# Splitting attention queries and keys where they are projected instead of where they are used

## The chip, the cores and the metric

The kernel runs on one core of a Trainium2 chip. The metric is the device time of one execution in microseconds (us). Before the change three executions took 3174.82, 3191.3 and 3205.16 us; the median is 3191.3.

## The reference, cut to what matters

One inference step of a one-layer trunk: a joint input projection, forgetting attention (8 heads of 64) and an mLSTM (4 heads of 128) side by side, an output projection, layer norm and a squared-ReLU MLP. It is done for a prompt of 2048 tokens and for 8 sequences of 8 sampled tokens whose keys and values lie in a paged cache of 8192 tokens each. All is float32. The part around the change is the prompt's attention:

```python
z = jnp.einsum('bsd,dc->bsc', x, w_in)
fq = z[..., OFF_FOX_Q:OFF_FOX_K].reshape(B, S, FOX_HEADS, FOX_HEAD_DIM)
fk = z[..., OFF_FOX_K:OFF_FOX_V].reshape(B, S, FOX_HEADS, FOX_HEAD_DIM)
...
L = jnp.cumsum(logf, axis=1).transpose(0, 2, 1)
...
s = jnp.einsum('bqhd,bkhd->bhqk', q_i, k).astype(jnp.float32) * scale
s = s + L_i[..., :, None] - L[:, :, None, :]
s = jnp.where(k_pos[None, :] <= q_pos[:, None], s, -jnp.inf)
p = jax.nn.softmax(s, axis=-1)
return jnp.einsum('bhqk,bkhd->bqhd', p.astype(v.dtype), v)
```

The keys `fk` are an output of their own too (`k_prompt`).

## The kernel before

**Three terms for one product.** Where float32 accuracy is wanted, an operand `x` is split into `hi` (rounded to the format fp32r) and `lo = x - hi`. `split_hi` (L154) is a copy on ScalarE, `split_lo` (L157) a subtraction on VectorE. `mm3` (L163 to L165) multiplies hi by hi, hi by lo and lo by hi.

**Phases.** Phase A (`block_a`) projects the tokens in four blocks of 512 (the first block with the 64 sampled tokens as well), in passes over columns of `w_in`: values and gates of the mLSTM, its queries and keys with a short convolution, output gates, then the attention's queries and keys (loop from L610, `j` 0 to 3 queries, 4 to 7 keys), then its values. For queries and keys a tile of PSUM has 128 columns by up to 512 tokens. In L632 to L635 ScalarE copies it in pieces of 256 tokens to `st` (queries scaled by 1/8) and SP's queue stores each piece: queries to the scratch tensor `dq` in DRAM, keys to the output `k_prompt`. PSUM tiles of this pool rotate over four banks.

Beside phase A run, woven in by `tick`, the mLSTM (`m_block`) and the attention over the cache (`sample_attention`), whose gathers are DMAs of the POOL queue: keys `kT` (L2109), values `vt`, `vx` or `y` (L2221); TensorE uses them in L2132 and L2245. `m_block` loads the end-of-chunk decays `gsb` (L738) and takes their exponential on ScalarE right away (L741), ahead of the loop over chunks; `gsb` is used in L793, at the end of a chunk. The gates `gm` are copied in L463; `m_load` (L714) waits for them with its load of `Wq`.

**Phase B** (`phase_b`, from L976) is the prompt's attention, in 64 units: 8 heads `h` by 8 groups `g` of 256 queries. The main loop does `scores` of unit n and then `values` of unit n - 1 (`LA = 1`).

- Keys: `keys_load` fetches 64 rows by 512 tokens twice, into both halves of the 128 partitions of `kn`; `keys` makes `ks` of it, hi on partitions 0 to 63 and lo on 64 to 127 (one `split_hi`, one `split_lo` on half the partitions). One matmul with `qh` on both halves then gives `qh*(hi + lo)`. Two tensors `ks0`, `ks1` of 2048 tokens alternate between heads.
- Queries: `queries_load` fetches 64 rows by 256 tokens twice into `qn`, two units ahead; `queries` makes `qh` and `ql`, one unit ahead.
- Scores: two matmuls (L1042, L1043) per query tile and 512 keys into a bank `pS` (three in turn); VectorE adds the negative cumulated forget gate `nl` while it copies the scores to `S` and takes the row maximum (L1050, L1054). For the tile on the diagonal the addend is `nd = nl + mask`, made on POOL (L1035) just before it is used, three buffers.
- Values: ScalarE takes the exponential (L1071), TensorE transposes (L1087), ScalarE or VectorE copies to `PT` (L1090, L1092), TensorE multiplies by the values `vn` (L1097) into `po`, which goes to `ot` (L1105, L1107). `nl` (1 MB, broadcast over partitions) and `vn` (512 KB, in rows of 256 bytes) of a head are loaded whole (`forget_values`, L984, L985) at g = 3 of the head before; head 0's come in quarters.
- `ot` holds 64 rows by 1024 queries, two buffers. When a half of a head is through, `finish` puts three steps into the list `ends`, of which the main loop does one per unit: `stores` of the inverse sums to DRAM (L1122), `sums`, which loads them broadcast (`rl`, L1128), and `scale`, two multiplications `ot*rl` and their stores to `dmix` (L1133, L1134). They run on POOL and SP's queue; at the very end (`end`) the first of the two runs on VectorE and the stores are POOL's, and the list is emptied in one go.

**Order.** The program is written in the order above, but each engine's order is made by a scheduler that simulates a timeline (`schedule_with_timeline_sim=True`): an instruction whose operands and buffer are there may go ahead of earlier ones. Each engine and queue then takes its instructions in the order so made, so an issue on SP's queue that waits has the later loads and stores behind it. POOL issues the cache gathers and, in phase B, the sums of weights of the MLP (`w2_sum`, L1242).

**Behind phase B** the output projection `phase_o` loads operands from `dmix` (`mix`, `xr`, L1318), splits them (`mh`, `ml`), loads residual rows `y` (L1345) and weights `w_o` in pieces (`half_wo`, L1247: five buffers `wr`, split into `wh`, `wl` for the first half of the columns and `woh`, `wol` for the second), and multiplies in L1359. Its tiles lie in memory that phase B used.

```python
ends.extend([stores, sums, scale])
while end and ends:
    ends.pop(0)()
```

## Time and profile before

| what | us |
|---|---|
| median of three executions | 3191.3 |
| the profiled execution | 3166.91 |
| its span, first to last instruction | 3165.1 |
| TensorE busy in the span | 3076.4 |
| phase A, to the first scores | 864.9 |
| phase B, first scores to last values | 440 |
| the rest: output projection, MLP | 1860 |

PE is TensorE's matmul, PEld its loading of the stationary operand, DVE is VectorE, ACT is ScalarE, POOL is GpSimd, and SP is the engine that issues most DMAs; a `q` behind an engine's name stands for its sequencer, which waits and issues. A group row reads: line, engine, operation, `out<-in` by the program's names, shape, count, then busy us and mean ns of one, then the idle us of the engine just before them and what ended it. A row of a window gives the stretch, its length, each engine's busy us (and instructions), the granted share of TensorE's clock, the mean busy share of the 16 DMA engines and GB/s. A row of waits reads: who waited, for whom, us in total, times, the longest. A row of a timeline gives start, duration, engine, line, operation and, in brackets, the idle time before it and what ended it; neighbours of one kind are merged (`x4`).

### The profile page before, as it was taken

The page shows a single profiled execution, that of the slowest core. Times are in us where ns is not written, and L with a number is a line of the kernel's source. Part 1 is how long each engine was busy: PE and PEld are TensorE (multiplying, and loading weights), DVE is VectorE, ACT ScalarE, POOL GpSimd, SP SyncE. Part 2 cuts the span into 40 slices and gives each one's busy share as a digit, 9 for nine tenths or more (in the row PEclk, how much of TensorE's full clock was granted, in tenths as well). Part 3 has the DMA queues.
Part 4 walks back from the last instruction along what each step waited for, and adds up shares of the span by engine and source line. Part 5 has one row for each costly group of instructions (what it writes and reads, how often), then busy time and mean ns, then how long its engine had stood idle before and what let it go on. Part 6 is the DMA issues. An engine that isn't in the chain of part 4 may idle for free.

```text
span 3165.1 us, 53757 instructions
## 1 busy us (share of the span) xinstructions
PE 3076.4 (97%) x19713; PEld 2425.7 (77%) x19713; DVE 2125.0 (67%) x5095; ACT 1457.3 (46%) x2648; POOL 961.5 (30%) x1046
## 2 busy tenths in 40 slices
PE   8999999999999999899999999999999999999998
PEld 8997787787766676677777777776777776798886
DVE  6857557466487888544566668665676656787888
ACT  4343244334377777422334354443454444455552
POOL 0121232333333334376423334324333222111110
PEclk9999999999999999999999999999999999999999
DMA  5565775777787787487977778978778866587772
GB/s 193 152 212 179 238 234 188 277 267 250 238 269 196 210 211 172 159 303 261 359 277 271 279 274 302 344 263 315 282 280 325 317 226 238 156 266 200 210 203 77
DMA packets 332512, 765.36 MB, mean 242 GB/s; under 512 B 64057, under 2 KB 154681, under 8 KB 331353
## 3 DMA queue, kind: packets, MB, share of 16 engines
q1 hardware_dynamic: 236120, 414.41, 39.9%
q0 software_dynamic: 90864, 330.61, 31.4%
q10 hardware_dynamic: 5264, 16.91, 1.4%
q8 instruction: 156, 2.56, 0.3%
q14 instruction: 108, 0.88, 0.1%
HBM read 709.23 MB, written 93.98 MB: 254 GB/s over the span
## 4 chain that ended last, share of the span: by engine, by line
PE 76%; DMA 11%; issue 5%; DVE 5%; POOL 2%; ACT 1%; SPq 0%; DVEq 0%; POOLq 0%; ACTq 0%
PE py L163 6%; PE py L165 6%; PE ph L163 6%; PE ph L165 6%; PE py L164 6%; PE ph L164 6%; PE pw L1359 5%; PE pm L163 5%; PE pm L165 5%; PE pm L164 5%; DMA y<-cache_v,idxV 3%; PE sO L2245 3%; PE po L1097 3%; DMA vt<-cache_v,idxV 3%; PE sQ L2132 3%
## 5 line engine op out<-in xcount | busy, mean ns | idle before, releaser
L157 DVE TENSOR_TENSOR wl<-wr,wh 128x1024 fp32r<-128x1024 f32 x321 | 393.5, 1230 | 237.3 <-ACT wh L154 235.7
L154 ACT ACTIVATE wh<-wr 128x1024 fp32r<-128x1024 f32 x321 | 337.6, 1055 | 326.0 <-PE ph L164 168.9
L2109 POOL DMA_INDIRECT kT<-cache_k,idxK x256 | 276.5, 1080 | 642.7 <-PE sQ L2132 576.4
L163 PE MATMUL py<-wh,hh 128*128 128x512 f32 x904 | 357.6, 400 | 0.1
L164 PE MATMUL py<-wl,hh 128*128 128x512 f32 x904 | 353.7, 393 | 0.0
L165 PE MATMUL py<-wh,hl 128*128 128x512 f32 x904 | 352.6, 394 | 0.8 <-DVE hl L157 0.8
L1668 DVE TENSOR_TENSOR y<-y,py 128x512 f32<-128x512 f32 x404 | 272.4, 681 | 84.5 <-PE py L165 81.4
L163 PE MATMUL ph<-x1h,wh 128*128 128x512 f32 x768 | 303.8, 396 | 0.0
L2221 POOL DMA_INDIRECT vt<-cache_v,idxV x197 | 203.2, 1032 | 329.8 <-PE sO L2245 257.4
L164 PE MATMUL ph<-x1l,wh 128*128 128x512 f32 x768 | 301.5, 393 | 0.0
L165 PE MATMUL ph<-x1h,wl 128*128 128x512 f32 x768 | 299.9, 393 | 0.0
L163 PE MATMUL pm<-xh,whi 128*128 128x512 f32 (+2 forms) x640 | 231.0, 361 | 0.0
L165 PE MATMUL pm<-xh,wlo 128*128 128x512 f32 (+2 forms) x640 | 228.8, 357 | 0.0
L164 PE MATMUL pm<-xl,whi 128*128 128x512 f32 (+2 forms) x640 | 227.9, 356 | 0.0
L163 PE MATMUL pm<-whi,xh 128*128 128x256 f32 (+4 forms) x624 | 202.1, 325 | 8.0 <-ACT whi L154 8.0
L157 DVE TENSOR_TENSOR wlo<-wra,whi 128x1024 fp32r<-128x1024 f32 (+1 forms) x112 | 141.0, 1261 | 101.1 <-ACT whi L154 100.8
L163 PEld LDWEIGHTS py<-wh,hh 128*128 128x128 f32 x904 | 169.4, 188 | 50.0 <-issue 5.9
L165 PEld LDWEIGHTS py<-wh,hl 128*128 128x128 f32 x904 | 170.1, 188 | 41.5 <-issue 4.9
L164 PE MATMUL pm<-wlo,xh 128*128 128x256 f32 (+4 forms) x624 | 199.5, 320 | 0.6 <-DVE wlo L157 0.6
L165 PE MATMUL pm<-whi,xl 128*128 128x256 f32 (+4 forms) x624 | 199.9, 320 | 0.0
L164 PEld LDWEIGHTS py<-wl,hh 128*128 128x128 f32 x904 | 170.5, 189 | 35.2 <-issue 2.5
L154 ACT ACTIVATE hh<-hq 128x512 fp32r<-128x512 f32 x150 | 94.1, 631 | 215.4 <-PE py L164 150.6
(442 smaller groups left out, 7210.5 us busy)
## 6 DMA issues: line engine op xcount, KB each, us to landing
wr<-w SPq DMA_DIRECT2D x214, 512.0 KB
wra<-w_in SPq DMA_DIRECT2D x104, 512.0 KB
wr<-dw SPq DMA_DIRECT2D x97, 512.0 KB
dw<-w POOLq DMA_DIRECT2D x63, 512.0 KB, 8.6
wr<-w POOLq DMA_DIRECT2D x34, 512.0 KB, 8.4
Rb<-dR SPq DMA_DIRECT2D x128, 128.0 KB
wx<-dw SPq DMA_DIRECT2D x17, 512.0 KB
xn<-xp_t SPq DMA_DIRECT2D x16, 512.0 KB
```

Of the source, the lines that this page charges most:

```text
L154: last["ACT"] = A.activation(dst, src, AF.Copy, scale=scale)
L157: r = (eng or V).tensor_tensor(dst, src, hi.bitcast(F32), op=OP.subtract)
L163: T.matmul(ps, wh, xh, start=first, stop=False, skip_group_check=shared)
L164: T.matmul(ps, wh, xl, start=False, stop=False, skip_group_check=shared)
L165: last["PE"] = T.matmul(ps, wl, xh, start=False, stop=stop, skip_group_check=shared)
L1097: last["PE"] = T.matmul(po[c:c + 64, q0:], z["vn"][:, k], PTs[k // 4][:, k % 4, q0:], start=(k < 2), stop=(k >= nk - 2), skip_group_check= ...
L1359: last["PE"] = T.matmul(ps, m[t][x][:, k], (wh, wl)[w][hf][k], start=i == 0, stop=i == 23)
L1668: V.tensor_tensor(y, y, ps, op=op)
L2109: G.indirect_dma_start(out=piece(n), out_offset=None, in_=ck, in_offset=IO(ap=idxK[:, b, j // 2, j % 2:j % 2 + 1], axis=0))
L2132: r = T.matmul(pq[h4 * 32:h4 * 32 + 32, hg].rearrange("p (k c) -> p k c", k=2), z["qb"][:, hd], kv, start=(db == 0), stop=(db == 1), skip_ ...
L2221: vx["last"] = G.indirect_dma_start(out=vt.rearrange("p f c -> p (f c)"), out_offset=None, in_=cv, in_offset=IO(ap=idxV[:, b, (kt % 4) * 4 ...
L2245: after_ = T.matmul(po[r:r + 32], z["PT"][:, hg, 2 * f + g, pg].rearrange("p h q -> p (h q)"), vts[f][:, g, hg * 256:(hg + 1) * 256], star ...
```

## The change

1. The projection stores queries and keys already split. ScalarE makes `hi` from PSUM (512 tokens at once where the tile has them), VectorE `lo` in one operation out of PSUM (`ps*scale - hi`), and SP stores both: queries to `dq[2, 512, S]`, keys to a new scratch tensor `dk[2, 512, S]`. The output `k_prompt` is still written as before, by its own two copies. The staging tiles are those that the convolution and the wide passes use (`ac`, `qi`).
2. Phase B loads the split form: `keys_load` brings hi and lo straight into `ks`, `queries_load` brings hi and lo of 256 queries into both halves of the partitions. `keys`, `queries` and their splits are gone. Five buffers `q` take the place of `qn`, `qh`, `ql`; loads run up to four units ahead.
3. `diagonals` makes a unit's two `nd` one unit ahead, with six buffers; for the first two units on VectorE.
4. `forget_values` of the next head comes in four pieces, at g = 4 to 7.
5. `ot` has three buffers, `ends` has an empty step between `sums` and `scale`, and at the very end both multiplications run on VectorE.
6. `gsb`'s exponential is taken in the first chunk of a block, after its outputs, instead of ahead of the loop.

```diff
-    dq = drm.tile([4, 128, S], F32, name="dq")
+    dq = drm.tile([2, 512, S], F32, name="dq")
+    dk = drm.tile([2, 512, S], F32, name="dk")
...
-                for o in range(w % 256, w, 256):
-                    st = pa.tile([128, 256], F32, name="st", bufs=4)
-                    A.activation(st, ps[:, o:o + 256], AF.Copy, scale=scale)
-                    SY.dma_start(O["k_prompt"][jj * 128:(jj + 1) * 128, a:a + 256] if c else dq[jj, :, a:a + 256], st)
+                n = w // 256 * 256
+                two = [lambda: pa.tile([128, 512], F32, name="sa", tag="ac", bufs=2),
+                       lambda: pa.tile([128, 512], F32, name="sq", tag="qi", bufs=2)]
+                if w == 512:
+                    hi, lo = (x().bitcast(F32R) for x in two)
+                else:
+                    x = two[w == 256]().bitcast(F32R)
+                    hi, lo = x[:, :256], x[:, 256:]
+                A.activation(hi, ps[:, w - n:], AF.Copy, scale=scale)
+                V.scalar_tensor_tensor(lo, ps[:, w - n:], scale, hi.bitcast(F32), op0=OP.mult, op1=OP.subtract)
+                for d, x in enumerate((hi, lo)):
+                    SY.dma_start((dk if c else dq)[d, jj * 128:(jj + 1) * 128, a:a + n], x.bitcast(F32))
+                for o in range(w - n, w, 256):
+                    if c:
+                        st = pa.tile([128, 256], F32, name="st", bufs=4)
+                        A.copy(st, ps[:, o:o + 256])
+                        SY.dma_start(O["k_prompt"][jj * 128:(jj + 1) * 128, a:a + 256], st)
                     a += 256
...
-        A.activation(gsb, gsb, AF.Exp)
         for c in range(bi * 4, bi * 4 + 4):
...
+            if c % 4 == 0:
+                A.activation(gsb, gsb, AF.Exp)
             Cn = pm.tile([128, 4, 129], F32, name="Cs", bufs=2)
...
+        def keys_load(z, g):
+            h = z["h"]
             for d in range(2):
-                SY.dma_start(kn[d * 64:d * 64 + 64], kp[h * 64:h * 64 + 64, g * 512:(g + 1) * 512])
-            return kn
+                SY.dma_start(z["ks"][g][d * 64:d * 64 + 64].bitcast(F32), dk[d, h * 64:h * 64 + 64, g * 512:(g + 1) * 512])
...
+            q = qs.pop() if qs else pb.tile([128, 2, 256], F32R, name="q", bufs=5)
+            for d in range(2):
+                SY.dma_start(q[d * 64:d * 64 + 64].bitcast(F32), q_of(*units[n]))
+            return q
...
+        def diagonals(n):
             h, g = units[n]
+            for qt in (2 * g, 2 * g + 1):
+                nd = nds[h, qt] = pb.tile([128, 128], F32, name="nd", bufs=6)
+                x = Z[h]["nl"][:, qt * 128:qt * 128 + 128]
+                if n < 2:
+                    V.tensor_tensor(nd, x, dmask, op=OP.add)
+                else:
+                    last["POOL"] = G.tensor_tensor(nd, x, dmask, op=OP.add)
...
-                z["ot"] = pb.tile([64, 1024], F32, name="ot", bufs=2)
+                z["ot"] = pb.tile([64, 1024], F32, name="ot", bufs=3)
...
-                    (V if end and q == 0 else G).tensor_tensor(ot[:, s], ot[:, s], rls[q], op=OP.mult)
+                    (V if end else G).tensor_tensor(ot[:, s], ot[:, s], rls[q], op=OP.mult)
...
-            ends.extend([stores, sums, scale])
+            ends.extend([stores, sums, lambda: None, scale])
...
+                if n + 1 < len(units):
+                    diagonals(n + 1)
                 if ends:
                     ends.pop(0)()
-                if n + 2 < len(units):
-                    qnext[n + 2] = queries_load(n + 2)
...
+                while max(qnext) < min(n + 4, 2 * n + 3, len(units) - 1):
+                    m = max(qnext) + 1
+                    qnext[m] = queries_load(m)
...
+                if h < 7 and g >= 4:
+                    forget_values(Z[h + 1], g * 512 - 2048, 512)
```

More of the change, by code (lines that the diff above doesn't have):

```diff
@@ L1030, in scores @@
                 mx = pb.tile([128, 8], F32, name="mx", bufs=6)
-                nd = pb.tile([128, 128], F32, name="nd", bufs=3)
-                if z["h"] == 0 and g < 2:
-                    V.tensor_tensor(nd, nl[:, qt * 128:n], dmask, op=OP.add)
-                else:
-                    last["POOL"] = G.tensor_tensor(nd, nl[:, qt * 128:n], dmask, op=OP.add)
+                nd = nds.pop((z["h"], qt))
                 st = []
@@ L1153, in phase_b @@
         dmask = bf["mask"]
-        keys(Z[0], 0, bf["kn"])
+        forget_values(Z[0], 0, 512)
+        nds = {}
+        diagonals(0)
         sc = {}
-        qnext = {1: queries_load(1)}
-        knext = {}
+        qnext = {0: bf["q"], 1: queries_load(1), 2: queries_load(2)}
         w2_due = [0.0]
```

95 lines of the change are left out of this document (34 added, 61 removed).

## The prediction

> **What bounds the kernel now.** I read the page first, then stretches of the span, then the waits of TensorE, then the places where these lie.
>
> ```profile
> span 3165.1 us, 53757 instructions
> PE 3076.4 (97%) x19713; PEld 2425.7 (77%) x19713; DVE 2125.0 (67%) x5095; ACT 1457.3 (46%) x2648; POOL 961.5 (30%) x1046
> q1 hardware_dynamic: 236120, 414.41, 39.9%
> ```
>
> TensorE is busy for 97%, and the change removes no matmul. It can win only what TensorE idles, or runs at a lower granted clock, near the code that it touches. The attention over the prompt (phase B) lies from 864.9 to 1304.9 us:
>
> ```profile
> core 0: us, PE busy (x) PEld busy (x) DVE busy (x) ACT busy (x) POOL busy (x), PEclk, DMA share, GB/s
> 864.90:904.90 40.00, 34.43 (x195) 22.73 (x196) 33.88 (x138) 29.26 (x71) 11.79 (x18) 0.91 0.74 207
> 1004.90:1024.90 20.00, 17.26 (x113) 12.34 (x113) 11.04 (x40) 11.12 (x25) 4.94 (x7) 0.91 0.69 152
> 1044.90:1064.90 20.00, 17.22 (x103) 11.60 (x103) 15.90 (x55) 12.25 (x29) 9.01 (x14) 0.91 0.75 205
> 1144.90:1184.90 40.00, 40.00 (x283) 28.82 (x282) 32.93 (x132) 29.01 (x68) 16.95 (x25) 1.00 0.90 222
> 864.90:1304.90 440.00, 422.22 (x2882) 296.64 (x2883) 352.14 (x1379) 331.42 (x769) 163.31 (x251) 0.98 0.75 199
> 1317.60:1337.60 20.00, 11.07 (x52) 7.79 (x52) 4.27 (x4) 3.17 (x3) 2.42 (x3) 0.83 1.03 402
> ```
>
> The fourth row shows the stage without trouble: all busy, full clock. Three stretches lose: idle 5.57, 2.74 and 2.78 us, and 0.09 of the clock, which is 3.6, 1.8 and 1.8 us. Over phase B that is 17.8 us of idle and 7.2 us of clock: **25 us is the most that B can give back.** The last row lies behind B, where the output projection starts: 8.9 us idle and 0.17 x 20 = 3.4 us of clock.
>
> **Phase B, part by part.** What TensorE waits for there:
>
> ```profile
> PE pt L1087 <- DVE PT L1092: 3.2, 4, 2.4
> PE pS L1042 <- DVE mx L1050: 2.8, 2, 1.4
> PE po L1097 <- DVE ot L1107: 2.7, 1, 2.7
> ```
>
> *Splits.* The splitting of queries and keys leaves B:
>
> ```profile
> L157 DVE TENSOR_TENSOR ql<-qn,qh 128x256 fp32r<-128x256 f32 x64 | 36.6, 579 | 4.1 <-ACT qh L154 3.8
> L157 DVE TENSOR_TENSOR ks<-kn,ks 64x512 fp32r<-64x512 f32 x32 | 23.5, 766 | 0.6
> L154 ACT ACTIVATE qh<-qn 128x256 fp32r<-128x256 f32 x64 | 26.6, 417 | 17.1 <-DMA qn<-dq 7.2 <-PE po L1097 4.9 <-PE pS L1042 3.6
> L154 ACT ACTIVATE ks<-kn 128x512 fp32r<-128x512 f32 x32 | 18.1, 624 | 2.0 <-DMA kn<-k_prompt 2.0
> ```
>
> VectorE loses 36.6 + 23.5 = 60.1 us of 352, ScalarE 44.7 of 331. Neither sets the pace where TensorE is full. They do so in the first 40 us, where the keys of two heads are split and VectorE is busy 33.9 of 40. Most of the 9.2 us lost there follows VectorE or ScalarE; the first exponentials cannot be hidden at all. Bounds 0 and -9.2; I take **-5**.
>
> The stretch at 1045 has one cause:
>
> ```profile
> 1051.81 3.20 DVE L157 TENSOR_TENSOR ql<-qn,qh 128x256 fp32r<-128x256 f32 x1
> ...
> 1055.67 0.66 PE L1087 MATMUL pt<-ident,S 128*128 128x128 f32 x4 [2.41 <-DVE PT L1092]
> ```
>
> A subtraction that takes 0.58 on average took 3.20 here, the copy behind it on VectorE came late, and TensorE idled 2.41 us for it. With the subtraction gone this goes: 2.78 + 1.8 = 4.6 at most, **-4**.
>
> *Values in pieces, third buffer, one more step.* The stretch at 1005:
>
> ```profile
> 991.87 0.54 SPq L985 DMA_DIRECT2D vn<-v_prompt  x1
> 994.18 16.89 SPq L1134 DMA_DIRECT2D dmix<-ot  x1
> ```
> ```profile
> ACT ot L1105 <- DMA dmix<-ot: 5.0, 1, 5.0
> ```
>
> Behind the 512 KB load of values the next issue on SP's queue, the store of a finished half, took 16.89 us. The buffer `ot` came free late, ScalarE waited 5.0 us, and TensorE 2.7. A third `ot`, loads in quarters and queries four units ahead each loosen this chain: 2.74 + 1.8 at most, **-4**. Of the other 6.7 us of scattered idle I take **-1.5**.
>
> *New.* Queries now come as two tensors: 128 loads of 128 KB instead of 64 KB, 8.4 MB more; queue 1 spent 0.399 x 3165 / 414 = 3.05 us of all engines per MB, so 26 us in 440, and the DMA share goes from 0.75 to 0.81. Scores now wait for a load with no split between. The nearest row is ScalarE's idle time before `qh`, 7.2 us for the load `qn`; between 0 and those 7.2 (four units of lead against two, five buffers) I take **+3.5**. The keys are loaded straight into the buffer that TensorE reads for the head before last: the load waits on SP for that head's last scores, and behind it on SP stand loads of queries and the steps of `ends`. It was so for the split that wrote the buffer, only on ScalarE; SP had three buffers of raw keys between. I count this wait into the 3.5, since the queries behind it are four units early.
>
> SP issues 42 more loads of values and forget gates (0.54 us each by the row above, 23 us of SP's queue), and they wait for the values of the head before last as the whole load did; nothing while the queries lead. The diagonals are the same 128 additions, asked for a unit earlier with six buffers for three; nothing. B: -5 - 4 - 4 - 1.5 + 3.5 = **-11**.
>
> **Behind B.** The last scaling moves from POOL to VectorE (`V if end else G`).
>
> ```profile
> 1300.78 14.70 SPq L1345 DMA_DIRECT2D y<-x_prompt  x5
> ...
> 1302.41 0.68 DVE L1133 TENSOR_TENSOR ot<-ot,rl 64x512 f32<-64x512 f32 x1 [1.62 <-DMA rl<-drl]
> ...
> 1305.61 9.04 POOL L1133 TENSOR_TENSOR ot<-ot,rl 64x512 f32<-64x512 f32 x1 [1.63 <-DVE pad_5x L85]
> ...
> 1306.60 4.62 DVE L157 TENSOR_TENSOR wl<-wr,wh 128x1024 fp32r<-128x1024 f32 x4
> ...
> 1316.01 2.44 SPq L1247 DMA_DIRECT2D wr<-w_o  x3
> ```
> ```profile
> 1330.14 1.22 PE L1359 MATMUL pw<-woh,mh 128*128 128x512 f32 x2 [8.89 <-ACT woh L154]
> ```
>
> Of the last two scalings one took VectorE 0.68 us and the other held POOL for 9.04, to 1314.65. The residual rows `y` are loaded into memory that its tiles occupied, so SP's issues of them lasted until 1315.48; the output weights `wr` stood behind them on SP, from 1316.01, and TensorE idled 8.89 us for what is made of them. With both scalings on VectorE, the second ends near 1306.3 and SP comes to the weights near 1307.5. Their buffers come free one by one as `wl` is made (first about 1307.8, with the added 0.68 about 1308.5): 7.5 us earlier than now. What is late next is the transfer itself, since the DMA share behind B is 1.03; it has idle time ahead of it instead. Bounds 0 and -(8.9 + 3.4) = -12.3. I take 7.4 of the idle and 2.3 of the clock, less 0.7 of VectorE in front of the weight splits: **-9**.
>
> **The projection (phase A).** Each tile of queries or keys now gets one ScalarE copy and one VectorE subtraction out of PSUM, and keys also the two old copies. The four stretches:
>
> ```profile
> 137.50:200.00 62.50, 62.50 (x500) 62.50 (x499) 45.69 (x175) 22.58 (x55) 18.67 (x22) 1.00 0.70 221
> 349.50:405.00 55.50, 52.46 (x285) 39.99 (x284) 23.68 (x64) 14.92 (x33) 13.50 (x15) 0.97 0.73 250
> 555.00:620.00 65.00, 62.90 (x405) 48.75 (x403) 28.75 (x88) 21.36 (x51) 25.23 (x28) 0.97 0.81 286
> 767.50:826.00 58.50, 57.20 (x391) 46.28 (x390) 28.05 (x101) 27.18 (x73) 20.75 (x26) 1.00 0.74 263
> ```
> ```profile
> 843.68 0.68 DVE L759 SCALAR_TENSOR_TENSOR Wq<-mm,Wq 128x512 f32<-128x512 f32 x1
> ```
>
> By the last row (the same operation, a PSUM source) the subtractions are at most 40 x 0.68 = 27 us of VectorE in 241.5 us where it works 126; ScalarE, busy 86, gets less. Both hide behind TensorE: four PSUM buffers rotate, so a finished tile may stay for three tiles' time, and the added work takes less than a tile. On SP the stores wait for VectorE's half and the weight loads of the next columns stand behind them, as they stand behind the old stores. Stores grow by 12.6 MB (queries 4.2, keys 8.4): 38 us of all DMA engines, 9.6 in each stretch, so the shares rise to 0.85, 0.90, 0.96 and 0.90. Room is left, little of it. TensorE's waits for gathered cache pieces in A:
>
> ```profile
> PE sO L2245 <- DMA vt<-cache_v,idxV: 3.4, 3, 1.8
> ...
> PE sQ L2132 <- DMA kT<-cache_k,idxK: 2.1, 2, 1.3
> ```
>
> Bounds 0 and +38 (all of it on the path); nearest is this row, 5.5, which I let grow by half: **+3**.
>
> The moved exponential `gsb` gives something back:
>
> ```profile
> 378.64 7.69 DMA gsb<-dgs
> ...
> 389.15 9.69 DMA Wq<-dMa
> ```
> ```profile
> 401.02 0.66 PE L769 MATMUL mm<-ident,qk 128*128 128x128 f32 x4 [3.04 <-ACT ot L698]
> ```
>
> ScalarE stood behind that load, the load of `Wq` followed late, and TensorE idled 3.04 us; the granted clock of that stretch is 0.97 (0.03 x 55.5 = 1.7). Bounds 0 and -4.7; **-4**. A: -1.
>
> **Sum:** -11 - 9 - 1 = -21: span 3144. The profiled execution took 3166.9, 1.8 around its span, and lies 24 below the median of the three runs (3191.3; 3174.8 to 3205.2). I carry the difference to the median: **3170**.
>
> A rule against part of this: the Trainium skill, "TensorE: Matmul & The Clock Gate", section "Why this matters for your kernels", asks that TensorE's gaps stay under about 3 us lest the clock fall. By it the gaps of 2.4 and 2.7 us would cost no clock and the sum would be 3.6 smaller, -17; the trace differs, with 0.91 granted in both stretches.
>
> **Rivals.**
> 1. *All waits go*: B -25, behind it -12, A -5: -42, **3149**. For: each named wait has a single cause which the change removes. Against: every transposition still waits for an exponential.
> 2. *The projection is held by DMA*: place, the four stretches; price, up to 38 us; it decides once a stretch's share passes 1. Then -21 - 3 + 38 = +14, **3205**, slower. For: 0.81 in the third stretch. Against: even there it comes to 0.96.
> 3. *The start of the output projection gains nothing.* The empty step in `ends` shifts the list by one: the scaling of head 7's first half has no unit left and runs in the loop at the very end, with the last one. If it stays there on POOL, the first operands wait for it.
>
> ```profile
> L1318 SPq DMA_DIRECT2D xr<-dmix x16: 359/417/1187, 1275.0 to 1477.8; - x16
> ```
>
> The first operand was loaded at 1275.0, 29 us ahead of its place in the program, so ready work is drawn forward; that speaks against it. Price: the 9 come back, **3179**, and a few us more if POOL is held again.
> 4. *B gains nothing*: the quarters block SP's queue four times a head, and queries or keys come late. Head 0's values already come in quarters, and behind one of them:
>
> ```profile
> 876.75 5.97 SPq L1010 DMA_DIRECT2D qn<-dq  x2
> ```
>
> Four times 5.97 is more than the one 16.89. Against it: 64 units in 440 us are 6.9 us each, so 5.97 is less than one unit of lead. Price: the 11 come back, **3181**. A page speaks for it: the Trainium skill, "DMA: Bandwidth & Descriptors", section "Bandwidth", wants DMAs of 1 MiB or more, and quarters go the other way; no run here shows its figure.
>
> **How the numbers follow.** Chances: forecast 0.55, rivals 0.15, 0.06, 0.14, 0.10. Single runs spread by 30 us, a median of three by perhaps 10 to each side, so under 1% cannot be told from no change; 1% is below 3159 or above 3223. Faster by over 1%: a fifth of the forecast (0.11) and most of rival 1 (0.11), 0.22. Slower: a sixth of rival 2 and 0.02 for what I overlooked, 0.03. The rest, 0.75, is the same. The range reaches past rival 1 (3149) with 2 and to just short of rival 2 with 3202.
>
> **What would show it.** Right: no `ql` or `ks` on VectorE in B, whose work there falls to about 292 us; B about 429 us long; no issue on SP's queue over 8 us; the gap ahead of the output projection's second weights under 3 us; no 3 us gap near 401. Wrong: TensorE waiting for `q` or `ks` loads, for `vt` or `kT` in the four stretches, or for the first `mh`; or B still near 440.

## The result, and the profile after

The changed kernel takes 3213.25 us (median of 11 runs) against 3191.3 for the kernel before on the same chip: a ratio of 1.0073, with a 95% interval of 1.0045 to 1.0100. It is slower by 0.7%, some 22 us, where 21 us faster had been forecast.

First the page of the changed kernel, then its stretches at places that answer to those of the prediction: the first 40 us of phase B, two places that will matter, phase B from its first scores to its last product with values, and the output projection behind it.

```profile
span 3214.8 us, 53745 instructions
PE 3095.7 (96%) x19713; PEld 2434.9 (76%) x19713; DVE 2086.0 (65%) x5040; ACT 1431.8 (45%) x2560; POOL 953.7 (30%) x1045
q1 hardware_dynamic: 254584, 435.38, 41.4%
```
```profile
867.10:907.10 40.00, 35.99 (x231) 24.44 (x230) 29.68 (x135) 26.93 (x63) 13.67 (x25) 1.00 0.85 242
1011.00:1041.00 30.00, 22.15 (x143) 15.26 (x142) 13.93 (x67) 14.11 (x35) 10.02 (x16) 0.89 0.79 181
1072.00:1092.00 20.00, 16.69 (x105) 12.40 (x105) 10.64 (x55) 11.74 (x30) 8.30 (x16) 0.83 0.59 170
867.10:1325.80 458.70, 421.77 (x2884) 302.55 (x2882) 300.24 (x1284) 302.11 (x676) 154.97 (x253) 0.97 0.78 208
1325.80:1552.40 226.60, 220.33 (x1390) 167.42 (x1390) 97.99 (x238) 56.59 (x84) 145.96 (x113) 0.98 0.85 290
```

The same two last stretches of the kernel before, cut at the same events:

```profile
864.90:1304.60 439.70, 421.92 (x2881) 296.38 (x2881) 351.90 (x1378) 331.12 (x769) 163.31 (x251) 0.98 0.75 199
1304.60:1533.10 228.50, 218.78 (x1390) 167.19 (x1390) 97.43 (x238) 56.79 (x84) 147.34 (x114) 0.99 0.80 284
```

Up to the end of the output projection the two profiles differ by 19.3 us (1552.4 against 1533.1), and phase B alone got 19.0 us longer, although VectorE does 52 us less in it and ScalarE 29 us less. TensorE is busy as long as before (421.8 against 421.9); what grew is its idle time, from 17.8 to 36.9 us. (The busy time hides something: TensorE's clock was halved for 30.7 us of B, where it was for 13.7 before.) The waits of TensorE in phase B say for whom:

```profile
PE pS L1047 <- DMA q<-dq: 25.0, 11, 4.8
PE pS L1047 <- DMA drl<-lt: 3.9, 1, 3.9
PE pt L1092 <- DVE PT L1097: 3.1, 3, 1.5
```

The first scores of a unit wait for the load of its queries. The second row is one more wait of this kind, for the first scores of head 6 at 1193.4 us: they wait for the semaphores of their two query loads, and the profile names an earlier DMA with one of these. So it is 28.9 us; the prediction allowed 3.5, 7.2 at most.

Three places behave as forecast. The first 40 us gain 1.56 us of TensorE and 0.09 of the clock. The wait near 401 us in phase A (3.04 us) is gone, and so is the wait of 8.89 us ahead of the second weights of the output projection, of which this is left:

```profile
349.50:405.00 55.50, 55.44 (x300) 41.91 (x299) 27.57 (x70) 15.62 (x30) 12.55 (x15) 1.00 0.85 297
...
1332.10 0.73 PE L1361 MATMUL pw<-wl,mh 128*128 128x512 f32 x2 [0.41 <-DVE wl L158]
```

The MLP and all else behind the output projection take 1632 us in the profile of before and 1662 in that of after. The change touches nothing there and TensorE's order there is the same. In the 16 experiments below this part takes 1642 to 1656 us in the first four, which shared one chip, and 1628 to 1635 in the others, whichever kernel it was. So these 30 us are not counted for the change: the two profiled spans differ by more than the medians do.

### The profile page after: what moved, and what is told of

Read it like the earlier page. It is cut to its first block, busy times and chain, and to the rows that moved or that the text cites. A ratio compares the mean times of both kernels' runs of the same rounds, so it can differ in the third digit from the quotient of the medians.

```text
span 3214.8 us, 53745 instructions
## 1 busy us (share of the span) xinstructions
PE 3095.7 (96%) x19713; PEld 2434.9 (76%) x19713; DVE 2086.0 (65%) x5040; ACT 1431.8 (45%) x2560; POOL 953.7 (30%) x1045
## 4 chain that ended last, share of the span: by engine, by line
PE 74%; DMA 12%; issue 5%; DVE 3%; POOL 2%; ACT 2%; another core or an unknown queue 1%; SPq 1%; DVEq 0%; ACTq 0%; POOLq 0%
PE py L164 6%; PE py L166 6%; PE ph L166 6%; PE ph L164 6%; PE py L165 6%; PE ph L165 6%; PE pw L1361 5%; PE pm L164 4%; PE pm L166 4%; PE pm L165 4%; PE sO L2247 3%; PE sQ L2134 3%; PE po L1102 3%; PE pt L1092 3%; DMA q<-dq 2%
## 5 line engine op out<-in xcount | busy, mean ns | idle before, releaser
L1055 DVE CUSTOM_DVE_ANT_0 S<-pS,nl 128x512 f32<-128x512 f32 (+3 forms) x288 | 166.5, 596 | 63.3 <-PE pS L1048 60.9
```

Source lines behind the costliest of these rows:

```text
L1055: last["DVE"] = V.tensor_tensor_reduce(out=sp[:, :e - a], in0=pS[:, :e - a], in1=nl[:, a:e], scale=1.0, scalar=NEG, op0=OP.add, op1=OP.max ...
```

## How the queries come late

SP's timeline around the first two long gaps, in the changed kernel (head 2 ends, head 3 begins; start, duration, line, what is issued, how often):

```profile
988.87 0.54 SPq L1139 DMA_DIRECT2D dmix<-ot  x1
989.45 1.70 SPq L1004 DMA_DIRECT2D nl<-dnl  x3
991.25 1.06 SPq L1005 DMA_DIRECT2D vn<-v_prompt  x2
992.41 11.81 SPq L1016 DMA_DIRECT2D q<-dq  x2
1004.32 5.20 SPq L1139 DMA_DIRECT2D dmix<-ot  x1
...
1018.53 1.11 SPq L1133 DMA_DIRECT2D rl<-drl  x2
1023.11 1.70 SPq L1139 DMA_DIRECT2D dmix<-ot  x2
1024.86 2.68 SPq L1016 DMA_DIRECT2D q<-dq  x4
```
```profile
1021.82 2.50 POOL L1138 TENSOR_TENSOR ot<-ot,rl 64x512 f32<-64x512 f32 x2 [20.66 <-ACT PT L1095]
...
1050.86 1.27 POOL L1138 TENSOR_TENSOR ot<-ot,rl 64x512 f32<-64x512 f32 x1 [19.01 <-DMA rl<-drl]
```
```profile
1015.71 0.36 PE L1047 MATMUL pS<-ks,q 128*128 128x256 f32 x1 [2.37 <-DMA q<-dq]
...
1033.89 0.76 PE L1047 MATMUL pS<-ks,q 128*128 128x512 f32 x1 [4.83 <-DMA q<-dq]
```

Two things make the loads late. First, the queue is slow to move what has been issued. Behind the pieces of the values the next two issues, queries of unit (3, 0), last 11.81 us, and the load lands 11 us after that; the store behind it lasts 5.20 us, although POOL had scaled its half by 991.4. TensorE is ready for the unit at 1013.3 and waits until 1015.7. What the queues moved in the 12 us of those issues can be counted (packets, MB, time that they took as a share of 16 engines; `q0` has the DMAs issued by POOL, here sums of weights in packets of 4 KB, `q1` those of SP):

```profile
q0 software_dynamic: 501, 1.81, 80.3%
q1 hardware_dynamic: 494, 0.88, 24.9%
```

One packet of SP's went for one of POOL's, whatever its size, and the engines were full. From 1004 to 1009 us it was 255 to 248, with most of SP's packets 256 bytes long.

Second, SP stands at a store that waits for another engine. The store of a scaled half (`dmix`, L1139) stands in SP's order ahead of the next query loads: it cannot go before POOL has scaled, POOL cannot scale before `rl` has landed (the later of its two rows names that load; at the earlier place it started 2.2 us after the second `rl` had been issued), and `rl` came from SP itself at 1018.5. From 1019.6 to 1023.1 SP issues nothing. Only then, at 1024.9, go the loads for units (3, 3) and (3, 4). TensorE is ready for (3, 3) at 1029.1 and waits until 1033.9, 8 us after those loads left. SP's waits at this line over all of B, by the profile's account (which also puts here stands of the queue like the 5.20 us above):

```profile
SPq L1139 <- POOL nd L1027: 28.4, 14, 3.8
SPq L1139 <- POOL ot L1138: 15.2, 5, 5.1
```

The kernel before stands at the same store for longer (59.2 and 22.9 us), with more lead to cover it. In the ten gaps of over 0.8 us the scores begin 0.14 us after their load has landed; these loads took 5 to 20 us from the end of their issue to landing, where the median of heads 2 to 7 is 5.0.

From the two timelines I worked out, for all units of heads 2 to 7, how long before its first scores the second half of a unit's queries was issued. Before, with loads "two units ahead": 12.7 to 39.3 us, median 22.8. After, with loads "four units ahead": 2.7 to 22.9 us, median 12.2. The lead got shorter. Too few buffers are not the reason, though the code suggests it: before, a raw buffer was free again as soon as it had been split, and three raw and three split buffers held six units; now one of five buffers comes back only with the last scores of its unit. But the same timelines show when a buffer came free and when SP issued the load into it. In the changed kernel the buffer lay free for 18.5 us in the median, never under 4.4; in the kernel before it was 4.0 (from the end of the split), with loads issued at once among them. SP was late, not the buffer. What a short lead costs depends on the units, which are not equal: undisturbed, the first four units of a head take 18.1 us together (1009.8 to 1027.9 in the run with stores on POOL and packed queries, below), not 4 x 6.9.

## The experiments

Theories, as the expectations name them. *P*: the four pieces of the values block SP's queue. *L*: too few query buffers that come back too late. *T*: the doubled bytes of the queries. *F*: SP's transfers take eight completion semaphores in turn, too few in flight. *A*: SP's queue has to share with the sums of weights that POOL's queue moves in packets of 4 KB, and so drains by its number of packets. *O*: SP's order, loads behind stores that wait. Each run is compared with runs of the kernel before on the same chip; "B" is the stretch from the first scores to the last product with values, "J" from there to the last product of the output projection, both in the profiled execution.

| run | B, us | J, us | ratio (95%) |
|---|---|---|---|
| before | 439.7 | 228.5 | 1 |
| changed | 458.7 | 226.6 | 1.0073 (1.0045 to 1.0100) |
| 1 values whole | 461.1 | 225.0 | 1.0050 (1.0032 to 1.0068) |
| 2 queries by ScalarE | 506.5 | 220.9 | 1.0186 (1.0166 to 1.0207) |
| 3 queries raw | 439.5 | 223.6 | 0.9967 (0.9949 to 0.9986) |
| 4 before, last scaling | 437.2 | 221.0 | 0.9969 (0.9952 to 0.9986) |
| 5 raw, twice the bytes | 474.8 | 219.6 | 1.0069 (1.0050 to 1.0088) |
| 6 packed, one load | 673.3 | 219.2 | 1.0715 (1.0695 to 1.0735) |
| 7 packed, two loads | 433.4 | 219.1 | 0.9977 (0.9962 to 0.9993) |
| 8 seven buffers | 453.7 | 219.9 | 1.0043 (1.0025 to 1.0061) |
| 9 changed, sums late | 414.4 | - | only B is read |
| 10 before, sums late | 426.0 | - | only B is read |
| 11 packed, values by POOL | 414.3 | 220.0 | 0.9903 (0.9873 to 0.9933) |
| 12 packed, stores by POOL | 411.1 | 218.6 | 0.9887 (0.9862 to 0.9911) |
| 13 changed, stores by POOL | 416.0 | 218.2 | 0.9901 (0.9884 to 0.9917) |
| 14 changed, values by POOL | 428.4 | 220.5 | 0.9967 (0.9954 to 0.9981) |
| 15 before, stores by POOL | 426.1 | 229.7 | 0.9954 (0.9935 to 0.9972) |
| 16 packed, both by POOL | 414.8 | 218.9 | 0.9891 (0.9874 to 0.9907) |

### One part undone, one part alone

**1. Values whole again.**

```diff
                 if h < 7 and g == 3:
                     head(Z[h + 1])
-                if h < 7 and g >= 4:
-                    forget_values(Z[h + 1], g * 512 - 2048, 512)
+                    forget_values(Z[h + 1], 0, S)
```

> The changed kernel, with the values and forget sums of the next head loaded whole in one step as before, not in four pieces. Theory P (the pieces): in the changed kernel the pieces leave SP's queue as a burst and hold the query loads of the next head's first units behind them (9.26 and 2.50 us for the two issues at 992.4); with one whole load the query gaps on TensorE fall from about 24 us to under 8, the head stretch from its first scores to its last sum goes from 458 to 440 us or less, and the time to a ratio of 0.999 to 1.002 with the kernel before. Theory L (lead): the loads come late because a query buffer is now given back only by the scores and because stores that wait for scaled sums stand ahead of the loads in the one queue; the pieces are not the cause, and the stretch stays at 453 to 463 us, the ratio at 1.004 to 1.010. Theory T (traffic): doubled query bytes; no change either, as for L.

B is 461.1 us, and TensorE waits 35.7 us for queries. P falls: whole or in pieces, the values hold the queue alike. L and T both foresaw that.

**2. Query loads by ScalarE.**

```diff
-                SY.dma_start(q[d * 64:d * 64 + 64].bitcast(F32), q_of(*units[n]))
+                A.dma_start(q[d * 64:d * 64 + 64].bitcast(F32), q_of(*units[n]))
```

> The changed kernel, with the query loads from the second on issued by ScalarE, not by SP; bytes, buffers and everything else as they are. Theories P and L (both hold that it is SP's order that makes the loads late): the gaps of TensorE that end on a query load fall from about 24 us to under 5, the stretch of the heads to 437 to 445 us, and the ratio to 0.998 to 1.003, against 126 more issues on ScalarE of about 0.6 us each (76 us beside 301 us of busy time in 458). Theory T (traffic: the transfers themselves are too slow): the gaps stay at 15 us or more wherever the loads are issued, the stretch stays at 450 us or above and the ratio at 1.005 or above.

```profile
PE pt L1092 <- ACT PT L1095: 59.0, 17, 9.8
PE pS L1047 <- DMA q<-dq: 8.1, 2, 6.2
```

Gaps on queries fell from 25.0 to 8.1 us (P and L said under 5), but an issue that stands still on ScalarE now holds ScalarE's own copies of `PT`, and TensorE waits 59.0 us for those. The run says where the wait went, not whose it was: no verdict on T.

**3. Queries raw, as before; all the rest of the change.**

```diff
+            qn = qs.pop() if qs else pb.tile([128, 256], F32, name="qn", bufs=3)
...
+                SY.dma_start(qn[d * 64:d * 64 + 64], dq[h // 2, h % 2 * 64:h % 2 * 64 + 64, g * 256:(g + 1) * 256])
...
+            split_hi(qh, qn)
+            split_lo(ql, qn, qh)
```

> The changed kernel, but with the queries as before: stored and loaded raw, two units ahead, split by ScalarE and VectorE into three pairs of buffers; keys split by the projection, diagonals one unit ahead, pieces of values and the third buffer of sums stay. Theory L (the query buffers): six units in flight again, so no gap on a query load; the stretch of the heads comes down from 458 to 430 to 440 us and the ratio to 0.993 to 1.000. Theory P (pieces and SP's order): the query loads still stand behind the pieces, and the gaps stay, now before the splits: the stretch stays at 448 us or above, the ratio at 1.002 or above. Theory T (bytes of queries): as for L, since the bytes go back as well.

B is back at 439.5 us and the whole at 0.9967, so the queries are the part that costs. L and T both foresaw it; run 5 tells them apart. VectorE works 26 us less in B than in the kernel before (325.6 against 351.9), and nothing of that reaches B here.

**4. The kernel before with the last scaling on VectorE, alone.**

```diff
-                    (V if end and q == 0 else G).tensor_tensor(ot[:, s], ot[:, s], rls[q], op=OP.mult)
+                    (V if end else G).tensor_tensor(ot[:, s], ot[:, s], rls[q], op=OP.mult)
```

> The kernel before, with one edit of the change alone: both scalings of the last head's second half on VectorE. The prediction's step: the wait of 8.89 us ahead of the output projection's second weights goes, and with it the 3.4 us of half clock, some 9 us: ratio 0.996 to 0.998, and the stretch from the last sum of the heads to the last product of the output projection goes from 228 to about 219 us. Rival: the wait goes, but the sample attention's work in that stretch (a wait of TensorE for the reciprocal sums on VectorE, 3.05 us in the changed kernel) or something later takes it up, and the stretch falls by 2 us or less, the ratio within 0.999 to 1.001.

J falls by 7.5 us and the whole by 0.31% (0.14 to 0.48). The rival falls. This part of the change is worth what was forecast.

### Bytes, packets, buffers

**5. Raw queries, each row loaded twice.**

```diff
-            qn = ... pb.tile([128, 256], F32, name="qn", bufs=3)
+            qn = ... pb.tile([128, 2, 256], F32, name="qn", bufs=3)
...
+                SY.dma_start(qn[d * 64:d * 64 + 64], dap(dq, h * 64 * S + g * 256, [[S, 64], [0, 2], [1, 256]]))
+            return qn[:, 0]
```

> As the run with raw queries (six units in flight, split on load), but each query load brings its rows twice, so that it moves the 128 KB of the changed kernel in as many packets of 1 KB; the second copy is read by nobody, and the masked diagonals have four buffers, not six, to make room. Theory T (traffic: twice the bytes of the queries): the stretch of the heads goes from the raw run's 439.5 us to 450 us or above, the ratio to 1.002 or above. Theory L (buffers given back late, not bytes): the stretch stays within 437 to 445 us, the ratio within 0.994 to 1.001, and TensorE waits under 5 us for queries.

```profile
PE po L1112 <- ACT PT L1105: 12.9, 3, 7.2
PE pS L1057 <- DVE mx L1065: 12.1, 6, 6.8
PE pt L1102 <- ACT PT L1105: 11.2, 11, 3.5
```

B goes from 439.5 to 474.8 us with six units of queries in flight: L alone does not explain it, and the added load on the queue does harm by itself. TensorE does not wait for a query here; it waits for ScalarE and VectorE, where the splits stand ahead of copies and row maxima and wait for the late load. ScalarE's idle time ahead of the splits shows this:

```profile
L155 ACT ACTIVATE qh<-qn 128x256 fp32r<-128x256 f32 x64 | 26.7, 417 | 79.9 <-DMA qn<-dq 68.9 <-PE pS L1057 6.1 <-PE pt L1102 4.0
```

**6 and 7. Hi and lo side by side in DRAM, packets of 2 KB in place of 1 KB; one load of 128 partitions, or two of 64.**

```diff
-    dq = drm.tile([2, 512, S], F32, name="dq")
+    dq = drm.tile([512, S // 256, 2, 256], F32, name="dq")
...
# 6
+            SY.dma_start(q.rearrange("p d c -> p (d c)").bitcast(F32), dap(dq, h * 128 * S + g * 512, [[0, 2], [2 * S, 64], [1, 512]]))
# 7
+                SY.dma_start(q[d * 64:d * 64 + 64].rearrange("p d c -> p (d c)").bitcast(F32), dap(dq, h * 128 * S + g * 512, [[2 * S, 64], [1, 512]]))
```

> The changed kernel, with the two halves of a query row side by side in DRAM, and one load of 128 partitions by 2 KB in place of two of 64 partitions by twice 1 KB: same bytes, half as many packets and half as many issues. Theory F (few loads in flight: SP's transfers take eight completion semaphores in turn, so an issue waits until the one eight before it has landed; 379 issues in the stretch of the heads): the waits of SP fall, the query gaps of TensorE go from 25 us to under 10, the stretch from 458 to 440 to 447 us, the ratio to 0.997 to 1.003. Theory L (a buffer comes back only with the scores): the lead of the loads grows by the issue time alone, gaps stay at 15 us or more, stretch 450 us or above. Theory T (time of the packets): gaps fall by about a fifth, stretch 452 to 456 us.

> As the run with one load for a unit's queries, but still two loads of 64 partitions by 2 KB: half the packets, as many issues as the changed kernel. Theories F and L: as the changed kernel, query gaps of 18 to 30 us, stretch 453 to 462 us, ratio 1.004 to 1.010. Theory T (time of the packets): gaps fall by about a fifth to a third, stretch 450 to 455 us.

TensorE's waits for queries, of run 6 and of run 7:

```profile
PE pS L1047 <- DMA q<-dq: 162.8, 28, 17.0
```
```profile
PE pS L1047 <- DMA q<-dq: 13.8, 9, 3.5
```

Run 6 is far off what any theory said and decides nothing among them; it is taken up at the end. Run 7 brings B from 458.7 to 433.4 us, more than T's 450 to 455, and against F and L. The queue's totals from the first scores to the last product with values, of the changed kernel and of run 7 (packets, MB, share of 16 engines; the expectations count in a window from 870 to 1300 us, which cuts off the end of the longer B):

```profile
q1 hardware_dynamic: 52616, 48.62, 37.9%
```
```profile
q1 hardware_dynamic: 44683, 48.54, 38.5%
```

The bytes did not fall, and the time that the engines spend on the packets hardly did (37.9% of 458.7 us is 174 us, 38.5% of 433.4 is 167). What fell is the number of packets, by 7933. This led to theory A.

**8. Seven query buffers, six units ahead; `ot` back to two buffers, without the empty step.**

```diff
-            q = ... pb.tile([128, 2, 256], F32R, name="q", bufs=5)
+            q = ... pb.tile([128, 2, 256], F32R, name="q", bufs=7)
...
-                z["ot"] = pb.tile([64, 1024], F32, name="ot", bufs=3)
+                z["ot"] = pb.tile([64, 1024], F32, name="ot", bufs=2)
```

> The changed kernel, with seven query buffers and loads six units ahead; for room the third buffer of sums goes back to two, and with it the empty step between the loads of the sums and the scaling. Theory L (too few buffers that come back too late): query gaps from 25 us to under 8, stretch of the heads 438 to 446 us, ratio 0.996 to 1.002. Theories F and T (SP's queue cannot issue, or move, the loads sooner): more buffers do not help, gaps stay at 15 us or more, stretch 450 us or above, ratio 1.003 or above.

```profile
PE po L1102 <- DVE ot L1112: 30.2, 4, 15.2
```

The waits for queries are gone, as L said, and B is 453.7 all the same (L said 438 to 446): now TensorE waits 30.2 us for `ot`, whose stores SP issues. Whatever has the least slack on SP's queue is what TensorE waits for. The queue is late, not one kind of load.

### The queue beside POOL's sums

**9 and 10. The 79 sums of weights after the last head, in the changed kernel and in the kernel before.**

```diff
-            while n and len(w2_done) < min(79, w2_due[0]):
+            while n == len(units) and len(w2_done) < 79:
```

> The changed kernel, with POOL's 79 sums of weights (its DMA queue's 512 KB transfers in packets of 4 KB) issued after the last head, not between the heads; what they feed comes late, so that only the stretch of the heads is read, not the whole time. Theory A (SP's packets take turns with POOL's: while sums run, SP's queue drains by its number of packets, whatever their size; the changed kernel has 49648 of them in the heads against 40170): the query gaps of TensorE fall from 25 us to under 5 and the stretch from 458 to 425 to 438 us. Theory O (SP's own order, its eight transfers in flight and its waits for stores): nothing of that changes, gaps of 10 us or more and a stretch of 446 us or above.

> The kernel before with the same edit, for comparison; again only the stretch of the heads is read. Theory A: it falls too, from 439.7 to 430 to 437 us (the two issues of 16.89 and 12.96 us behind the values get shorter), and stands 3 to 12 us above that of the changed kernel with the same edit: what the prediction had for the heads, once the queue is out of the way. Theory O: it stays at 436 to 441 us, and the changed kernel's stays above it.

B of run 9, two rows of its SP timeline, and B of run 10:

```profile
867.90:1282.30 414.40, 408.58 (x2883) 297.11 (x2880) 299.04 (x1283) 298.77 (x672) 116.85 (x196) 0.99 0.54 152
```
```profile
983.76 0.93 SPq L1005 DMA_DIRECT2D vn<-v_prompt  x2
984.79 1.26 SPq L1016 DMA_DIRECT2D q<-dq  x2
```
```profile
863.20:1289.20 426.00, 415.58 (x2881) 294.18 (x2881) 343.59 (x1377) 332.29 (x769) 123.33 (x191) 1.00 0.42 125
```

B of the changed kernel loses 44.3 us, to less than A expected, and the query gaps are gone; the lead of the loads is 16.5 to 31.7 us, and a free buffer waits 0.9 us for its load, not 18.5. The issue behind the pieces of values takes 1.26 us, not 11.81. SP's queue in the 8 us around it (984 to 992), with no packet of POOL's beside it:

```profile
q1 hardware_dynamic: 3108, 1.87, 89.1%
```

That is 389 packets per us, where the changed kernel moved 41 (494 in 12 us). So SP's queue drains by the number of its packets, at POOL's pace, while those sums run. SP still stands at its stores (52.6 us by the profile), and nothing is late by it. Theory O as put here, with a stretch of 446 us or above, falls. Run 9 also frees POOL itself of issuing the sums (116.85 us busy, 154.97 with them); that this is what helped is unlikely, since in run 13 POOL works longer than either, 173.33 us, and B is as short.

The kernel before falls too, to 426.0. The difference between the two kernels is 11.6 us in favour of the change; where it lies is taken up below. The Trainium skill, "DMA: Bandwidth & Descriptors", section "Queues, rings and completion order", has each DMA engine change between queues packet by packet; the counts above, 501 to 494, agree with it. (A packet of that page holds several descriptors; whether the profile counts the same unit is not shown here.)

**11 and 12. Packed queries as in 7, and the pieces of values (11) or the stores of the scaled sums (12) issued by POOL.**

```diff
# 11
-            SY.dma_start(z["vn"][:, a // 128:(a + n) // 128], vp[a:a + n, h * 64:h * 64 + 64].rearrange("(t p) c -> p t c", p=128))
+            G.dma_start(z["vn"][:, a // 128:(a + n) // 128], vp[a:a + n, h * 64:h * 64 + 64].rearrange("(t p) c -> p t c", p=128))
# 12
-                    (G if end else SY).dma_start(dmix[...], ot[:, s])
+                    G.dma_start(dmix[...], ot[:, s])
```

> As the run with packed queries in two loads, and the pieces of the values (packets of 256 bytes, 15872 in the heads) issued by POOL, not by SP; forget sums stay on SP. Theory A (the number of packets on SP's queue): SP's queue loses a third of its packets, the rest of the query gaps (12.8 us) falls to under 4, the stretch of the heads from 433.4 to 420 to 429 us, the ratio to 0.991 to 0.996. Rival: the pieces hold POOL up instead (masked diagonals and scalings behind them), and TensorE waits for those: stretch 432 us or above, ratio 0.997 or above.

> As the run with packed queries in two loads, and the stores of the scaled sums issued by POOL in all heads, so that SP no longer waits for POOL's scaling (25 and 14 us of SP's waits there). Theory O (SP's order: loads stand behind stores that wait): query gaps from 12.8 to under 5 us, stretch from 433.4 to 424 to 430 us, ratio 0.992 to 0.996. Theory A: SP's waits there cost nothing, since the queue's packets set the pace: stretch 431 to 436 us, ratio 0.996 to 0.999.

Run 11 went as A said. Run 12 did not: A gave 431 to 436 us, O 424 to 430, and B is 411.1, below both and the shortest of all, at 0.9887. So SP's order does matter, under the load that A names.

**13 to 15. The unpacked changed kernel with the stores alone (13) or the values alone (14) on POOL, and the kernel before with the stores on POOL (15).** The edits are those of 12 and 11.

> The changed kernel, with the stores of the scaled sums issued by POOL in all heads; queries unpacked, all packets as they are. Theory O (SP's order: query loads stand behind stores that wait for POOL's scaling): this alone takes the query gaps from 25 us to under 8 and the stretch of the heads from 458 to 425 to 438 us, ratio 0.991 to 0.998. Theory A (number of packets on SP's queue, beside POOL's): the gaps fall by no more than a third, stretch 446 us or above, ratio 1.002 or above. Both needed, one after the other: stretch 438 to 446 us.

> The changed kernel, with the pieces of the values issued by POOL; queries unpacked. Theory A (packets): SP's queue loses 15872 of its 49648 packets, twice what packing the queries takes away, so the stretch falls by at least as much as by packing (25 us), to 420 to 434 us, ratio 0.990 to 0.997. Theory O (stores that wait): SP still stands behind the stores, and the stretch stays at 442 us or above, ratio 1.000 or above.

> The kernel before, with the stores of the scaled sums issued by POOL in all heads. Theory O: the kernel before loses to the same wait (59.2 and 22.9 us of SP's waits), though its deeper buffers hide most; the stretch goes from 439.7 to 428 to 436 us, ratio 0.994 to 0.998. Theory A: 437 to 442 us, ratio 0.998 to 1.002.

TensorE's waits for queries in run 13, and B of runs 13 and 15:

```profile
PE pS L1047 <- DMA q<-dq: 0.7, 1, 0.7
```
```profile
871.00:1287.00 416.00, 408.86 (x2883) 296.43 (x2881) 299.34 (x1284) 302.53 (x676) 173.33 (x283) 1.00 0.85 229
```
```profile
861.50:1287.60 426.10, 417.37 (x2880) 295.66 (x2880) 351.20 (x1378) 333.09 (x769) 182.46 (x281) 0.99 0.78 205
```

Moving one line's stores off SP takes 42.7 us off B and turns 1.0073 into 0.9901, more than O foresaw (425 to 438 us). The bytes are the same, and SP's queue loses only 2370 of its 52616 packets by it, where packing took 7933 away for 25.3 us. Its place that answers to 1018.5 above:

```profile
1018.09 1.11 SPq L1133 DMA_DIRECT2D rl<-drl  x2
1019.25 2.56 SPq L1016 DMA_DIRECT2D q<-dq  x4
```

The loads for (3, 3) and (3, 4) now follow 1.2 us behind `rl`, not 6.3, and the scores of (3, 3) find their queries there. A's limit for run 13 (446 or above) falls, and so does O's for run 14 (442 or above), which went as A said (428.4). Both theories hold, since they are two sides of one loop: SP stands at a store until POOL has scaled, POOL waits for a load from SP's own queue, and that load takes its time by what the queue drains beside the sums. Take away the sums (9) or the store (13), and the loads are early enough; take away a part of the packets, and they are late less often (13.8 us of query gaps are left in run 7, 10.3 in run 14). In the kernel before the same move takes 13.6 us off B (15).

**16. Both on POOL, packed.** The edits of 11 and 12 together.

> Packed queries in two loads, with both the pieces of the values and the stores of the scaled sums issued by POOL. Either of the two alone left 4.6 and 5.9 us of idle TensorE in the heads (411.1 and 414.3 us), so both theories expect little: stretch 408 to 413 us, ratio 0.985 to 0.990. Rival: POOL's own order then holds up its diagonals or the stores, and the stretch is 414 us or above, ratio 0.990 or above.

B is 414.8 us, where 408 to 413 was expected and the rival said 414 or above; the ratio, 0.9891, is in the expected range. It is no sum of two gains, since little is left to gain. Run 12 has the lowest ratio, well below both kernels; runs 11, 13 and 16 cannot be told from it by the intervals, and run 13 is one line away from the changed kernel.

## Why the prediction was wrong

*The step that failed* is the paragraph "New" of phase B. It gave +3.5 us for "scores now wait for a load with no split between", with bounds of 0 and 7.2. The profile has 28.9 us of such waits, and with the halved clock that follows the gaps (0.89 and 0.83 in the two stretches shown) B is 19 us longer, not 11 shorter. In place of "four units of lead" the runs showed a queue that is late: SP issues a load 18.5 us after its buffer is free, because its packets go one for one with POOL's while POOL's sums run (without them, run 9, B is 414.4 us) and because it stands at stores that wait for POOL (without these, run 13, 416.0). Both halves of the reasoning were off. "Four units of lead against two" counted steps of the program; in us the lead fell from a median of 22.8 to 12.2. And the bound was no bound: ScalarE's 7.2 us ahead of `qh` were measured with that longer lead and with a split between load and use, so they say nothing of late loads without that cover.

*SP's added issues* were costed at "nothing while the queries lead". That named the cover and not what happens without it. The store that waits for POOL was read only for its effect on `ot`, not for what stands behind it on SP.

*Rival 4* ("the quarters block SP's queue ... and queries or keys come late") had the symptom and half of the cause: run 1 shows that the quarters are not to blame but the values as such (14), and its price ended at zero gain because 5.97 us was weighed against an average unit of 6.9.

*Traffic.* "The DMA share goes from 0.75 to 0.81" came out as 0.78; an average with room left said nothing of the 12 us at 992 in which the engines were full and SP's queue got every second packet.

*What held.* The splits left B as said: VectorE's work there fell to 300 us (292 forecast), and the first 40 us won 1.56 us of idle and 3.6 of clock (5 forecast). With the queue out of the way B wins 11.6 us (9 against 10), or 10.1 (13 against 15), close to the 11 of the forecast; but this is luck, since it is not won where forecast. The first head, which was to give 5, takes 48.1 us in run 9 and 48.0 in run 10, and the stretches near 1005 and 1045, which were to give 4 each, have nothing left to lose in run 10, where no gap after 930 us is over 0.9. The gain comes in every later head. Heads 4 to 6 of runs 10 and 9:

```profile
1068.81:1225.10 156.29, 154.35 (x1083) 110.16 (x1082) 129.49 (x519) 123.75 (x289) 40.58 (x63) 1.00 0.30 85
```
```profile
1067.60:1219.48 151.88, 151.88 (x1081) 110.96 (x1080) 111.80 (x481) 111.65 (x253) 37.04 (x63) 1.00 0.43 115
```

Both have full clock; 1.9 us of the 4.4 are idle time, the rest is TensorE's busy time itself, and what shortens it stays open. The prediction took a stretch with TensorE busy at full clock for one where nothing can be won. By this its ceiling was wrong too: "25 us is the most that B can give back", and run 12 has B 28.6 us below the kernel before.

Behind B, 9 us were forecast; the wait went, J fell by 7.5 us alone (4) and by 8.0 to 10.3 in runs 5 to 8, 11 to 14 and 16 (3.5, 7.6 and 4.9 in runs 1 to 3). In the profile of the changed kernel itself J fell only 1.9 us, as a new wait lies at its end, in the attention over the cache, with 6.8 us at half clock around it; it is absent from runs 7 and 13:

```profile
1517.47 1.94 PE L2134 MATMUL sQ<-kT,qb 128*32 128x256 f32 x16 [3.05 <-DVE rl L2193]
```

The scaling of head 7's first half (rival 3) held nothing up. In phase A the gain near 401 came (2.98 us of TensorE, 0.03 of clock), and the feared growth of the waits for gathered cache pieces did not:

```profile
PE sO L2247 <- DMA vt<-cache_v,idxV: 2.8, 3, 1.6
...
PE sQ L2134 <- DMA kT<-cache_k,idxK: 0.4, 1, 0.4
```

That is 3.2 us, where 5.5 were measured before and 8 were forecast. The length of phase A itself (864.9 before, 867.1 after) varies from 863.4 to 873.5 us over the runs with a split projection and from 861.5 to 870.7 over those with the old one, so its balance stays open to some 5 us.

## What to carry to other kernels

A prefetch distance is worth its us, not its steps: work it out from the trace as issue to use, at the shortest steps. Then compare the time at which a buffer comes free with the issue of the load into it: where the buffer lies free for long, the queue is late, and more buffers only cover that. On an in-order queue, look for issues that wait for another engine and see what stands behind them; a store that waits for work fed by that same queue belongs on another one. A split or copy between load and use is also a buffer, so removing it removes slack: a wait measured behind such cover is no bound for the wait without it. And where two queues share the engines, count packets, not bytes.

## What was not expected of the hardware

- *One load instead of two was the worst of all.* Run 6 moves the same bytes as run 7 in packets of the same size, with half as many issues, yet TensorE waits 162.8 us for queries, 17.0 at the longest, against 13.8 and 3.5. The source pattern begins with a dimension of 2 (step 0) in one, of 64 in the other. The Trainium skill, "DMA: Bandwidth & Descriptors", section "Rules for kernel authors", says that a leading dimension of c under 16 keeps a whole transfer on at most c of the 16 engines. The traces agree: a query load of run 7 raises its completion semaphore in 16 updates, one of run 6 in three, the first 0.42 us behind the issue and two when data lands, in the median 14.2 us behind it (5.0 in run 7). Another order of the dimensions was not tried.
- *Another queue helps where order is the trouble.* The same section says that spreading transfers over SP, ScalarE and POOL does not raise bandwidth and only saves issue time. No run here measures bandwidth alone, but the order of issues was worth more than their time: moving the stores saved 42.7 us of B (13), as nothing stood any longer behind them, and moving the values 30.3 (14), with 36004 packets left on SP's queue of 52616; and it cost 47.8 where the issues stood ahead of ScalarE's work (2).
- *Gaps and the clock.* By the rule weighed in the prediction, gaps under about 3 us cost no clock. In B the gap of 2.37 us at 1015.7 cost none, the one of 2.06 us at 1134.1 did, as the two stretches of the changed kernel below show. It depends on where a gap lies: in each of the 18 traces all stretches at half clock begin on one grid of 3.41 us. A line of the grid cuts the first gap into 1.48 and 0.89 us; the second lies whole between two lines. Counted over all traces behind their first 7 us, each of the 186 intervals of the grid at full clock with more than 2.0 us idle was followed by half clock, and 13 of the 16070 with less than 1.6 us were.

```profile
1012.00:1028.00 16.00, 12.98 (x98) 9.75 (x98) 9.77 (x50) 10.18 (x26) 6.18 (x11) 1.00 0.59 150
...
1132.00:1142.00 10.00, 7.94 (x49) 5.51 (x49) 2.98 (x19) 4.70 (x12) 0.80 (x1) 0.83 0.63 200
```

- *A queue can be late with room in the average share.* In B the 16 engines were busy 0.78 of the time, yet an issue behind 256-byte packets lasted 11.81 us; with POOL's sums away the same issue took 1.26. In those 12 us the engines were full, most of the time with POOL's packets (80.3% against 24.9%).
- *The packets' own time told little.* Half the packets per query load took 25 us off B, while the engines' time on SP's packets fell by 7 us.
